# Copies between PSUM banks queued right behind their source product, and another order of the products in two blocks of a Strassen FFN

## The chip, the cores and the metric

The kernel runs on one core of one Trainium2 chip. Its five engines work side by side, each through its own queue in the order in which the program issued: TensorE (PE; its weight loads are shown as PEld), VectorE (DVE), ScalarE (ACT), GpSimd (POOL) and SyncE (SP), which issues most DMAs. They wait for each other by semaphores. Matmul results land in PSUM, in banks of 512 float32 columns; everything else that an engine touches lies in SBUF. The metric is the time of one execution on the device in microseconds, lower is better. A kernel's time is the median of its runs.

## The reference

One decoder block for 512 tokens of width 2048 in float32: RMSNorm, one input projection, 16 attention heads of two kinds, a group norm, an output projection, then the part that the change touches, a SwiGLU feed-forward of 5632 hidden units, and a final norm.

```python
hn2 = rmsnorm(h, norm2_g[l])
h = h + (jax.nn.silu(hn2 @ w_gate[l]) * (hn2 @ w_up[l])) @ w_down[l]
return rmsnorm(h, final_g)
```

## The kernel before

**Three matmuls for one.** Float32 accuracy is kept by splitting each operand into a high part and a low part and multiplying high by high, low by high and high by low. On the weight side a half of a unit (128 partitions by 512 columns) is one *job*. `first` (L133) is ScalarE's copy into `wh` (L139), `second` (L141) VectorE's subtract into `wl` (L142). `wh` and `wl` have five buffers each. Some jobs have a `prep`, an add of VectorE ahead of `first` (L786), or a `post` behind `second`: an add, or the issue of a load. `next_half` (L177) is called by every half just before its matmuls; it issues the split three halves ahead (`first` of job i+3, `second` of job i+2), then whatever `later(n, f)` (L188) has put off to this half. A piece of work that is put off is therefore queued behind the splits that were issued before it.

**The FFN.** The hidden units are worked in 44 blocks `f` of 128. For each block the gate and up projections of the 512 tokens are computed together by a Strassen scheme: instead of eight products there are seven, P1 to P7, each of 256 columns and two halves, 24 matmuls (`product`, L1037). A product's weights are sums of the quarters A11, A21, A22, A12 of the block's weights; the sums are made in place by VectorE, two 512-column adds each. P1 and P7 use PSUM tag "proj", P4 and P6 "sc", P5 "o". P2 adds into P1's bank and P3, from block 1 on, into P6's bank. Two banks are seeded, from block 1 on: before P6 runs, ScalarE copies P1 into P6's bank (L1084), and before P7 runs, it copies P6 into P7's bank (L1090). The seeded products then accumulate on top, so their first matmul waits for the copy.

**The order.** `ORDER` (L831) is P1, P4, P6, P5, P7, P2, P3 for blocks 1 to 43; block 0 has `ORDER0`. The list `sched` (L842 on) fixes the order of all products. In every fourth block, 4 to 40, sixteen units `d` of the down projection follow its third to sixth product, four after each (`down`, L1115, 24 matmuls each, banks `pd` or P3's). The last four blocks' down projection is done in `last` (L1176).

**What a product leaves behind.** `after` (L1067) issues what must be done with a finished product. For blocks from 1 on it is put off by one half (L1174), so it is queued in the second half of the product that follows. After P3 come two VectorE operations (L1109, L1112 with the add of L1073) and `finish`: Silu on ScalarE (L1057), a multiply by VectorE (L1060), a copy by ScalarE (L1061) and a subtract (L1065). After P2 comes a multiply out of P1's bank (L1104), after P7 a copy (L1100) and two VectorE operations (L1073, L1076).

**Around blocks 1 and 2.** After P5 in block 1 and in block 2, eight halves in a row each issue one `put_away` (L1134): VectorE multiplies a tile of the residual (L1135), and SP stores its 256 KB to DRAM (L1136). In blocks 41 and 42 the tiles are brought back (L1146). The raw weights have five buffers of a quarter each; the load of a quarter of the next block is issued by the post of P6, of P7 (two) or of P3 (L819 to L822) and starts when the buffer it gets is free.

**Two offsets.** `wh` and `wl` of a half start 16 columns into their buffers, or 32 for halves marked `even` (L122); in the FFN that is the first half of P1 in blocks 1, 2 and those with f % 8 = 5 (L827).

Of the kernel before, what the change touches and what calls it, by code (L numbers as in the profile page):

```python
# [13 lines left out]
AF = mybir.ActivationFunctionType  # L14
# [57 lines left out]
def block_kernel(ctx: ExitStack, tc: tile.TileContext, xt, wst, wdn, smalls, wg, w2c, bias, ident_in, out):  # L72
# [3 lines left out]
    pe, act, dve, pool_e, sp = nc.tensor, nc.scalar, nc.vector, nc.gpsimd, nc.sync  # L76
# [28 lines left out]
    def load_to(n):  # L105
        while state["dma"] < min(n, len(units)):
            u = state["dma"]
            t = wp.tile([128, 1024], F32, tag="raw", name="raw", bufs=RB)
            for k in range(2 if u < TWO else 1):
                c = slice(512 * k, 512 * k + 512) if u < TWO else slice(0, 1024)  # L110
                sp.dma_start(t[:, c], wst[u][:, c])
            raws[u] = t
            state["dma"] += 1
            if units[u] == ("quad", 0, 1):
                pool_e.dma_start(t, wst[u + 1], accum_op=OP.add)
# [72 lines left out]
    def later(n, f):  # L188
        i = len(lag)
        while i and lag[i - 1][0] > pos["half"] + n:  # L190
            i -= 1
        lag.insert(i, (pos["half"] + n, f))
# [65 lines left out]
    def tokens(*accs):  # L258
        return [[a[:, 128 * t:128 * t + 128] for a in accs] for t in range(accs[0].shape[-1] // 128)]
# [46 lines left out]
    for k in range(KB):  # L306
        x = xc.pop(k)
# [417 lines left out]
    for j in range(NH):  # L725
# [9 lines left out]
        o = {}  # L735
# [42 lines left out]
    def quad_jobs(f, order):  # L778

        u = base_u + 4 * f  # L780

        def q(i, k):
            return raws[u + i][:, 512 * k:512 * k + 512]

        def comb(o, x):
            return lambda: dve.tensor_tensor(o(), o(), x(), op=OP.add)  # L786

        def fetch(o, i, k):

            return lambda: pool_e.dma_start(o(), wst[u + i][:, 512 * k:512 * k + 512], accum_op=OP.add)  # L790

        def nxt(i):
            return lambda: load_to(u + 4 + i + 1)

        r = {}
        for k in range(2):
            A11, A21, A22, A12 = (lambda i=i, k=k: q(i, k) for i in range(4))

            if f == 0:
                r["P1", k] = Job(A11, load=None if k else nxt(-1), post=fetch(A11, 1, k))  # L800
                r["P5", k] = Job(A21, post=fetch(A21, 0, k))
                r["P7", k] = Job(A11)
                r["P2", k] = Job(A12)
                r["P4", k] = Job(A22, prep=comb(A12, A21))
                r["P6", k] = Job(A21)
                r["P3", k] = Job(A12)
            else:
                r["P1", k] = Job(A11, post=comb(A11, A21))
                r["P4", k] = Job(A22, post=comb(A21, A22))
                r["P6", k] = Job(A22, prep=comb(A22, A11))  # L810
                r["P5", k] = Job(A21)
                r["P7", k] = Job(A11)
                r["P2", k] = Job(A12)
                r["P3", k] = Job(A12, prep=comb(A12, A22))
        if f + 1 < FB:
            if f == 0:
                r["P6", 1].post = nxt(2)
                r["P3", 1].post = nxt(3)
            else:  # L819
                r["P6", 1].post = nxt(0)  # L820
                r["P7", 1].post = nxt(2)
                r["P3", 1].post = nxt(3)  # L822
        else:
            r["P6", 1].post = lambda: load_fin(1)
            r["P5", 1].post = lambda: load_fin(2)
            r["P3", 1].post = lambda: load_fin(LA)
        r["P1", 0].even = f in (1, 2) or f % 8 == 5  # L827
        return [r[p, k] for p in order for k in range(2)]

    ORDER0 = ("P1", "P5", "P2", "P7", "P4", "P6", "P3")  # L830
    ORDER = ("P1", "P4", "P6", "P5", "P7", "P2", "P3")  # L831

    def dn_job(p, nb):
        return Job(lambda: dn[p, nb], post=load_dn)

# [5 lines left out]

    sched = []  # L842
    for f in range(FB):
        qj = quad_jobs(f, ORDER if f else ORDER0)
        p = f // PH - 1
        nb = 0
        for i, name in enumerate(ORDER if f else ORDER0):
            sched.append(("q", f, name))
            jobs += qj[2 * i:2 * i + 2]
            if f and f % PH == 0 and i > 1:  # L850
                for _ in range(4):
                    if nb < KB:
                        sched.append(("d", p, nb))
                        jobs.append(dn_job(p, nb))
                        nb += 1
# [84 lines left out]
    def ft(name="ft"):  # L940
        return ffn.tile([128, S], F32, tag="ft", name=name, bufs=2)
# [82 lines left out]
    for n in range(8):  # L1024
# [4 lines left out]
    banks = {n: ps.tile([128, 512], F32, tag=t, name=n, bufs=2)  # L1029
             for n, t in (("P1", "proj"), ("P7", "proj"), ("P4", "sc"), ("P6", "sc"), ("P3", "t"))}  # L1030
# [4 lines left out]
    st = {}  # L1035
# [31 lines left out]
    def after(f, name):  # L1067

        def x(k):
            return st[k][:, :256]  # L1070

        def add(o, a, b):
            dve.tensor_tensor(o, a, b, op=OP.add)  # L1073

        def sub(o, a, b):
            dve.tensor_tensor(o, a, b, op=OP.subtract)  # L1076

        g, u = st.get("g"), st.get("u")
        if name == "P1":
            st["g"] = ft()  # L1080
            if f:
                st["u"] = ft()
                st["P6"] = banks["P6"]
                act.activation(x("P6"), x("P1"), AF.Copy)  # L1084
            else:
                act.activation(st["g"][:, LO], x("P1"), AF.Copy)
        elif name == "P6":
            if f:
                st["P7"] = banks["P7"]
                act.activation(x("P7"), x("P6"), AF.Copy)  # L1090
                act.activation(u[:, LO], x("P4"), AF.Copy)
                return
            add(g[:, HI], g[:, LO], x("P6"))
            dve.tensor_tensor(g[:, LO], x("P1"), st["r2"][:, LO], op=OP.mult)
            add(u[:, LO], g[:, HI], x("P7"))
            add(u[:, HI], u[:, LO], x("P5"))
            sub(u[:, LO], u[:, LO], x("P4"))
            add(g[:, HI], g[:, HI], x("P5"))
        elif name == "P7":
            act.activation(g[:, HI], x("P5"), AF.Copy)  # L1100
            sub(u[:, LO], x("P7"), u[:, LO])
            add(u[:, HI], x("P7"), g[:, HI])
        elif name == "P2":
            dve.tensor_tensor(g[:, LO], x("P1"), st["r2"][:, LO], op=OP.mult)  # L1104
            if f == FB - 1:
                finish(f, g, u, LO)
        elif name == "P3":
            if f:
                add(g[:, HI], x("P6"), g[:, HI])  # L1109
            else:  # L1110
                add(g[:, HI], g[:, HI], x("P3"))
            dve.tensor_tensor(g[:, HI], g[:, HI], st["r2"][:, HI], op=OP.mult)  # L1112
            finish(f, g, u, HI if f == FB - 1 else slice(0, 512))
# [28 lines left out]
    def bring_back(nb):  # L1142
        if nb == 0:
            st["dnp"].close()
            st["hs"] = ctx.enter_context(tc.tile_pool(name="fin", bufs=1)).tile([128, KB, S], F32, name="hs")
        sp.dma_start(st["hs"][:, nb, :], kept_sums[nb])  # L1146

    for kind, a, b in sched:
        if kind == "d":
            down(a, b)  # L1150
            continue
        f, name = a, b
        product(f, name)
        if name == "P5" and f in (1, 2):
            for n in range(8):
                later(n, lambda nb=8 * (f - 1) + n: put_away(nb))
        if name == "P5" and f in (FB - 3, FB - 2):
            for n in range(8):
                later(n, lambda nb=8 * (f - FB + 3) + n: bring_back(nb))
        if f == 0:  # L1160
            if name == "P7":
                r = st["rs2"] = Rsqrt(tokens(sacc), D, rab.v[:, :4])
                r.invert()
                dve.tensor_tensor(r.z, r.z, rab.y[:, :4], op=OP.mult)
                later(1, lambda r=r: st.update(inv=Spread(r.z, True), r2=Spread(r.y)))
            if name == "P6":
                st["inv"] = st["inv"](False)
                act.activation(st["rs2"].rs[:, 7, :1], ones[:, :1], AF.Silu)
                st["r2"] = st["r2"](tag="t", bufs=2)
                st["u"] = ft()  # L1170
            if name in ("P1", "P6", "P3"):
                later(0 if name == "P1" else 1, lambda name=name: after(0, name))
        elif name in ("P1", "P6", "P7", "P2", "P3"):
            later({(FB - 1, "P2"): 0, (FB - 1, "P3"): 3}.get((f, name), 1), lambda f=f, name=name: after(f, name))  # L1174
# [150 lines left out]
```

## Time and profile before

| | us |
|---|---|
| median of 3 runs | 2255.78 (2252.54 to 2259.78) |
| the profiled execution | 2250.55 |
| its span, first to last instruction | 2248.7 |
| from P1 of block 1 to P1 of block 4 | 71.38 |
| from P1 of block 4 to the last matmul of the blocks | 1258.16 |

How the lines are read: a group has its line, engine, operation, what it writes and reads, the count, then the engine's busy time and the mean duration, then the idle time of the engine before it and what ended most of that. In the waits a row says who waited for whom, for how long in total, how many times, and the longest. In the timeline a row is start, duration, engine, line, operation; square brackets give the idle time before it and what ended it. In a table by windows a row is the window, its length, then for each engine busy time and number of instructions, the granted TensorE clock, the share of the DMA engines and GB/s. Ends of matmuls are modelled; their starts are not.

### The profile page before, as it was taken

Reading aid. Unit: us, or ns where it says so; the run is one execution under the profiler, and the core shown is the slowest. Engines: PE = TensorE matmul, PEld = TensorE weight load, DVE = VectorE, ACT = ScalarE, POOL = GpSimd, SP = SyncE. Lnnn points to the kernel's source line nnn. Section 1 sums busy time; section 2 is a strip of 40 time slices with the busy share of each in tenths; the row PEclk is TensorE's granted clock in tenths of the full one; section 3 lists DMA queues with packets and bytes.
Section 4 is the critical chain, followed back from the end, with each engine's and each line's share of the span. In section 5 each row is a group of like instructions: output and inputs, shape, how many; then the busy total and the mean of one; then the engine's idle time right before and its main releaser. Section 6 shows DMA issues by size and latency. Waiting matters only on the chain.

```text
span 2248.7 us, 40167 instructions
## 1 busy us (share of the span) xinstructions
PE 2203.7 (98%) x15776; PEld 2058.1 (92%) x15776; DVE 1451.5 (65%) x2796; ACT 1080.5 (48%) x2155; POOL 181.4 (8%) x211
## 2 busy tenths in 40 slices
PE   9999999999999998999999999999999999999998
PEld 7888888888888888999999999999999999999997
DVE  6765555455667689758384856657484847667486
ACT  6544444344453455445454545445454545445456
POOL 0000000000000000010201011010202010010203
PEclk9999999999999999999999999999999999999999
DMA  6432222222224344572836465473737365463752
GB/s 226 161 119 82 87 78 75 97 78 87 78 94 154 100 104 140 137 166 94 176 111 148 120 151 131 124 160 98 172 107 177 104 146 137 124 140 100 158 194 94
DMA packets 109517, 282.64 MB, mean 126 GB/s; under 512 B 11920, under 2 KB 14608, under 8 KB 109328
## 3 DMA queue, kind: packets, MB, share of 16 engines
q1 hardware_dynamic: 85424, 236.49, 33.3%
q0 software_dynamic: 23760, 43.53, 12.7%
q8 instruction: 123, 2.02, 0.4%
q14 instruction: 66, 0.54, 0.1%
q10 hardware_dynamic: 144, 0.07, 0.0%
HBM read 229.70 MB, written 50.33 MB: 125 GB/s over the span
## 4 chain that ended last, share of the span: by engine, by line
PE 86%; DVE 7%; issue 4%; ACT 3%; ACTq 0%; DVEq 0%
PE P L1050 12%; PE P L1051 12%; PE P L1052 11%; PE pp L170 7%; PE pp L172 7%; PE pp L171 7%; PE pd L1050 4%; PE pd L1052 4%; PE pd L1051 4%; PE pab L170 3%; PE pab L171 3%; PE pab L172 3%; DVE wl L142 3%; DVE raw L786 1%; ACT wh L139 1%
## 5 line engine op out<-in xcount | busy, mean ns | idle before, releaser
L139 ACT ACTIVATE wh<-raw 128x512 fp32r<-128x512 f32 x888 | 545.5, 627 | 482.1 <-PE P L1051 185.0
L142 DVE TENSOR_TENSOR wl<-raw,wh 128x512 fp32r<-128x512 f32 x888 | 602.1, 687 | 176.8 <-ACT wh L139 170.5
L1050 PE MATMUL P<-ah,wh 128*128 128x256 f32 x1552 | 437.4, 282 | 31.2 <-ACT P L1084 30.9
L1052 PE MATMUL P<-ah,wl 128*128 128x256 f32 x1552 | 432.2, 279 | 0.0
L1051 PE MATMUL P<-al,wh 128*128 128x256 f32 x1552 | 432.0, 278 | 0.0
L1050 PEld LDWEIGHTS P<-ah,wh 128*128 128x128 f32 x1552 | 291.7, 188 | 39.3 <-ACT P L1084 39.2
L1052 PEld LDWEIGHTS P<-ah,wl 128*128 128x128 f32 x1552 | 292.2, 188 | 0.0
L1051 PEld LDWEIGHTS P<-al,wh 128*128 128x128 f32 x1552 | 291.8, 188 | 0.0
L142 DVE TENSOR_TENSOR wl<-rawd,wh 128x512 fp32r<-128x512 f32 x160 | 110.7, 692 | 265.9 <-ACT wh L139 259.5
L170 PE MATMUL pp<-ah,wh 128*128 128x512 f32 x640 | 260.5, 407 | 0.0
L172 PE MATMUL pp<-ah,wl 128*128 128x512 f32 x640 | 250.9, 392 | 0.0
L171 PE MATMUL pp<-al,wh 128*128 128x512 f32 x640 | 250.2, 391 | 0.0
L786 DVE TENSOR_TENSOR raw<-raw 128x512 f32<-128x512 f32 x346 | 238.2, 688 | 6.5
L1130 POOL DMA_DIRECT2D sums<-stg x160 | 138.6, 866 | 1150.3 <-ACT stg L1129 1042.7
L1050 PE MATMUL pd<-ah,wh 128*128 128x256 f32 x784 | 217.8, 278 | 0.0
L1052 PE MATMUL pd<-ah,wl 128*128 128x256 f32 x784 | 217.7, 278 | 0.0
L1051 PE MATMUL pd<-al,wh 128*128 128x256 f32 x784 | 217.5, 277 | 0.0
L139 ACT ACTIVATE wh<-rawd 128x512 fp32r<-128x512 f32 x160 | 100.8, 630 | 222.2 <-PE pd L1051 84.3
L1052 PEld LDWEIGHTS pd<-ah,wl 128*128 128x128 f32 x784 | 147.2, 188 | 0.0
L1051 PEld LDWEIGHTS pd<-al,wh 128*128 128x128 f32 x784 | 147.1, 188 | 0.0
L1050 PEld LDWEIGHTS pd<-ah,wh 128*128 128x128 f32 x784 | 147.1, 188 | 0.0
L172 PEld LDWEIGHTS pp<-ah,wl 128*128 128x128 f32 x640 | 120.2, 188 | 28.3 <-DVE wl L142 0.4
(284 smaller groups left out, 4631.2 us busy)
## 6 DMA issues: line engine op xcount, KB each, us to landing
raw<-in_wst_dram SPq DMA_DIRECT2D x310, 512.0 KB, 4.0
rawd<-in_wdn_dram SPq DMA_DIRECT2D x160, 256.0 KB, 3.1
sums<-stg POOLq DMA_DIRECT2D x160, 256.0 KB, 4.5
bias<-in_bias_dram SPq DMA_DIRECT2D x16, 320.0 KB, 3.0
xc<-in_xt_dram SPq DMA_DIRECT2D x16, 256.0 KB, 3.0
hs<-in_xt_dram SPq DMA_DIRECT2D x16, 256.0 KB, 5.2
sums<-hs SPq DMA_DIRECT2D x16, 256.0 KB, 2.1
hs<-sums SPq DMA_DIRECT2D x16, 256.0 KB, 5.4
```

The source lines that it names most:

```text
L139: act.activation(self.h, self.src(), AF.Copy)
L142: dve.tensor_tensor(self.l, self.src(), self.h.bitcast(F32), op=OP.subtract)
L170: pe.matmul(o, wh, mh, start=start, stop=False)
L171: pe.matmul(o, wh, ml, start=False, stop=False)
L172: pe.matmul(o, wl, mh, start=False, stop=stop)
L786: return lambda: dve.tensor_tensor(o(), o(), x(), op=OP.add)
L1050: pe.matmul(o, wh, mh, start=start, stop=False, skip_group_check=True)
L1051: pe.matmul(o, wh, ml, start=False, stop=False, skip_group_check=True)
L1052: pe.matmul(o, wl, mh, start=False, stop=stop, skip_group_check=True)
L1130: pool_e.dma_start(kept_sums[nb], t, accum_op=OP.add)
```

## The change

The two copies L1084 and L1090 leave `after`. They are issued in the loop over `sched` directly behind the matmuls of P1 and of P6, ahead of the next half's splits, instead of in the second half of the next product. `ft()` for `g` and `u` and the copy of P4 (L1091) stay where they were. Blocks 1 and 2 get an order of their own, in which P2 is third: P1, P4, P2, P6, P5, P7, P3. In it P6, P5 and P7 are two halves later than before, and with them what hangs on them: their posts, and the `put_away`s that start from P5.

```diff
     ORDER = ("P1", "P4", "P6", "P5", "P7", "P2", "P3")
+    ORDER1 = ("P1", "P4", "P2", "P6", "P5", "P7", "P3")
+
+    def order(f):
+        return ORDER0 if not f else ORDER1 if f < 3 else ORDER
...
-        qj = quad_jobs(f, ORDER if f else ORDER0)
+        qj = quad_jobs(f, order(f))
...
-        for i, name in enumerate(ORDER if f else ORDER0):
+        for i, name in enumerate(order(f)):
...
             if f:
                 st["u"] = ft()
-                st["P6"] = banks["P6"]
-                act.activation(x("P6"), x("P1"), AF.Copy)
...
         elif name == "P6":
             if f:
-                st["P7"] = banks["P7"]
-                act.activation(x("P7"), x("P6"), AF.Copy)
                 act.activation(u[:, LO], x("P4"), AF.Copy)
                 return
...
+        if f and name in ("P1", "P6"):
+            o = {"P1": "P6", "P6": "P7"}[name]
+            st[o] = banks[o]
+            act.activation(st[o][:, :256], st[name][:, :256], AF.Copy)
```

## The prediction

> **What bounds the kernel now.** I read the page first, then the waits of TensorE, then a window table by stage, then the timeline of one block.
>
> ```profile
> span 2248.7 us, 40167 instructions
> PE 2203.7 (98%) x15776; PEld 2058.1 (92%) x15776; DVE 1451.5 (65%) x2796; ACT 1080.5 (48%) x2155; POOL 181.4 (8%) x211
> PE 86%; DVE 7%; issue 4%; ACT 3%; ACTq 0%; DVEq 0%
> ```
>
> TensorE sets the end: 98% busy and 86% of the chain. So a gain can come only from TensorE idling less or from its matmuls following each other more closely. The waits of TensorE (whole span first, then blocks 1 to 3, then block 4 to the end of the FFN, the last row for the weight loads in that last stretch) name one thing:
>
> ```profile
> PE P L1050 <- ACT P L1084: 30.9, 35, 3.3
> ...
> PE P L1050 <- ACT P L1084: 8.7, 3, 3.3
> PE P L1050 <- DVE ft L1104: 0.8, 2, 0.4
> ...
> PE P L1050 <- ACT P L1084: 22.2, 32, 1.0
> PEld P L1050 <- ACT P L1084: 29.9, 37, 1.2
> ```
>
> L1084 is the copy of P1 into P6's bank. P6 waits for it in nearly every block. The ends of matmuls are modelled, so the truer loss from block 4 on is the 29.9 us of the weight loads. The other moved copy, L1090, is waited for by nobody. Why L1084 is late shows in the timeline of block 19 (ScalarE and TensorE rows; P4 follows P1 at 1415.48):
>
> ```profile
> 1415.48 0.28 PE L1050 MATMUL P<-T4h,wh 128*128 128x256 f32 x1
> 1415.77 0.63 ACT L1057 ACTIVATE ft<-ft 128x512 f32<-128x512 f32 x1 [1.29 <-DVE ft L1112]
> 1416.45 1.16 ACT L139 ACTIVATE wh<-raw 128x512 fp32r<-128x512 f32 x2
> 1418.44 0.63 ACT L1061 ACTIVATE ah<-ft 128x512 fp32r<-128x512 f32 x1 [0.84 <-DVE ft L1060]
> 1418.98 0.37 ACT L1084 ACTIVATE P<-P 128x256 f32<-128x256 f32 x1
> 1418.09 0.28 PE L1052 MATMUL P<-T4h,wl 128*128 128x256 f32 x1
> 1419.40 0.38 PE L1050 MATMUL P<-ah,wh 128*128 128x256 f32 x1 [1.04 <-ACT P L1084]
> ```
>
> P1 is complete at about 1415.65 (its last matmul's modelled end). The copy starts 3.3 us later, because it is queued behind the Silu of the block before, two weight splits and L1061, which itself waits for VectorE. P6 could have followed at 1418.20 and starts at 1419.40.
>
> The second thing is how closely matmuls follow each other. In this window table a row's x counts two matmuls that had begun before the window:
>
> ```profile
> 858.74:930.12 71.38, 61.83 (x504) 60.88 (x505) 63.34 (x109) 32.77 (x60) 0.00 (x0) 0.98 0.46 148
> 905.99:930.12 24.13, 21.51 (x168) 21.30 (x169) 19.63 (x33) 10.92 (x20) 0.00 (x0) 0.93 0.44 143
> 930.12:2188.28 1258.16, 1235.69 (x10562) 1228.16 (x10561) 806.09 (x1319) 613.74 (x1122) 138.62 (x160) 1.00 0.56 138
> 1442.57:1496.97 54.40, 54.40 (x482) 54.40 (x481) 21.71 (x34) 24.16 (x45) 13.87 (x16) 1.00 0.86 182
> 939.47:996.00 56.53, 56.53 (x482) 56.53 (x481) 22.10 (x35) 24.35 (x45) 13.87 (x16) 1.00 0.81 175
> 997.43:1001.51 4.08, 4.08 (x38) 4.05 (x36) 3.77 (x8) 2.60 (x5) 0.00 (x0) 1.00 0.20 36
> 1001.66:1015.90 14.24, 14.24 (x121) 14.24 (x121) 11.43 (x19) 7.56 (x14) 0.00 (x0) 1.00 0.49 148
> 2188.28:2216.50 28.22, 28.22 (x242) 28.22 (x241) 18.18 (x39) 23.10 (x50) 10.42 (x12) 1.00 0.18 56
> ```
>
> The same 480 matmuls (16 down units, P5, P7, P2, P3) take 54.40 us in block 20 and 56.53 us in block 4: 113.3 ns against 117.8 ns, at the full granted clock and without a wait in either. There are two spacings. In block 5 the first half of P1, the one that the kernel places at the other offset, ends the wide one: after it 36 matmuls take 4.08 us, 113.3 ns. P6 then waits, and the next 120 take 14.24 us, wide again. In the starts of all matmuls of the FFN I find no change of spacing except at a TensorE wait or at such a half; a start after a wait falls into the wide spacing about two times in three. So each P6 wait costs twice: the wait, and the chance of a wide stretch behind it.
>
> **The change part by part.** The sum is made against the profiled execution: 2250.55 us, that is the span of 2248.7 and 1.85 around it. The median of the runs shown is 2255.78, 5.2 above; I add nothing for that, since which spacing falls out after each wait may well be what differs from run to run.
>
> *P1's copy right behind P1 (43 blocks).* No instruction is added; one of 0.37 us moves forward on ScalarE past two splits and L1061. In block 19 ScalarE reaches it when Silu ends, 1416.40, P1 being complete; it is done at 1416.77. P6 can start at 1418.20, so 1.4 us are to spare. What now stands behind the copy (the two splits, 1416.45 to 1417.61, and through VectorE's subtract also L1060 and L1061) slides by 0.37; the half that needs the first of them is P6's second, due at 1418.20 + 1.36 = 1419.56. Both splits end at 1417.98, a subtract of 0.69 (the row of 1421.68 below) at 1418.7 at the latest. Covered by 0.9 us; without that cover it would cost its 0.37. VectorE's subtracts and L1065 behind it are as early or earlier than their users by as much. So from block 4 on P6 waits for nothing.
>
> The stretch from block 4 to the end of the FFN has 40 x 7 x 24 + 160 x 24 = 10,560 matmuls. At 113.3 ns they take 1196.8 us of the 1258.16: 61.4 us are waits (29.9 by the weight-load row) and wide spacing (the other 31.5; if all were wide it would be 10,560 x 4.44 ns = 46.9). With no wait left, the half in block 5 sets the close spacing and nothing in the trace ends it: close stretches run through whole down stretches in blocks 12, 16, 20, 24 and 28 while DMA share is 0.86. What remains: block 4, before that half, at two chances in three of 552 x 4.44 ns = 2.45, 1.6; some 1.8 for the offset halves and jitter. Gain 61.4 - 3.4 = **58.0**; bounds 30 (waits alone) and 61.4. The tail's first 240 matmuls inherit the spacing, now 28.22 / 240 = 117.6 ns: **1.0** more, between 0 and 1.0.
>
> *P6's copy right behind P6.* L1090 gains nothing, nobody waits for it. It costs ScalarE a wait at its place. Block 19, from the second half of P6 on (a window of VectorE work first, then rows):
>
> ```profile
> 1420.87:1427.67 6.80, 6.80 (x63) 6.80 (x61) 4.95 (x8) 3.74 (x7) 0.00 (x0) 1.00 0.64 173
> ...
> 1421.01 0.63 ACT L139 ACTIVATE wh<-raw 128x512 fp32r<-128x512 f32 x1 [0.60 <-PE P L1051]
> 1421.68 0.69 DVE L142 TENSOR_TENSOR wl<-raw,wh 128x512 fp32r<-128x512 f32 x1 [0.46 <-ACT wh L139]
> 1426.31 0.28 PE L1050 MATMUL P<-ah,wh 128*128 128x256 f32 x1
> ```
>
> The split at 1421.01 will stand behind a copy that starts when P6 ends, three halves of 1.36 before the last row, about 1422.3: it moves to 1422.7, 1.7 us, and its subtract ends at 1424.1. Its half, P7's second, starts at 1426.31: 2.2 us of cover. Queued behind it on VectorE are the subtracts and adds of P7 to P3; VectorE is idle 6.80 - 4.95 = 1.85 us up to 1427.67, which takes up the 1.7 before its full stretch begins. Cost 0; without that cover 1.7 a block.
>
> [...]
>
> *Blocks 1 and 2, P2 third.* Nothing is added; P6, P5 and P7 run two halves later, and with them the posts of P6 and P7, the put-aways (eight multiplies and eight 256 KB stores from P5 on) and the next block's loads. P2 accumulates in P1's bank and so needs the copy first. The loads by line (us to landing last), and SP's rows:
>
> ```profile
> raw<-in_wst_dram SPq DMA_DIRECT2D x310, 512.0 KB, 4.0
> ...
> 869.08 2.13 SPq L111 DMA_DIRECT2D raw<-in_wst_dram  x2
> 872.89 3.92 SPq L1136 DMA_DIRECT2D sums<-hs  x3
> 876.85 0.43 SPq L111 DMA_DIRECT2D raw<-in_wst_dram  x1
> ```
>
> The first load waits for A21's subtract in P5 as now, the second for A11's in P7, about 1 us later; the third now stands behind one store, not three. The second, issued near 872 (SP's two rows of 869.08 end at 871.2, and 1 us), lands 4.0 later near 876; it is A22 of block 2, whose half starts near 881: hidden. Blocks 1 and 2 now, Silu and P6's start:
>
> ```profile
> 864.21 0.63 ACT L1057 ACTIVATE ft<-ft 128x512 f32<-128x512 f32 x1 [1.28 <-DVE ft L1112]
> 867.84 0.39 PE L1050 MATMUL P<-ah,wh 128*128 128x256 f32 x1 [3.32 <-ACT P L1084]
> 887.54 0.63 ACT L1057 ACTIVATE ft<-ft 128x512 f32<-128x512 f32 x1 [1.88 <-DVE ft L1112]
> 888.12 0.28 PE L1052 MATMUL P<-T4h,wl 128*128 128x256 f32 x1
> 891.17 0.39 PE L1050 MATMUL P<-ah,wh 128*128 128x256 f32 x1 [2.77 <-ACT P L1084]
> ```
>
> In block 1 the split of P2 needs no add of VectorE ahead of it, as P6's did, so L1112 and Silu come one operation, 0.6 us, earlier: Silu ends at 864.84 - 0.6 = 864.2 and the copy at 864.6. P4's modelled end is 867.84 - 3.32 = 864.5, P2 could follow 0.17 before that, so 0.3 is left of the wait. In block 2 Silu stays ahead of the copy and VectorE far behind, and four put-aways now fall into P1 and P4 of blocks 2 and 3 where two did. Counting VectorE's queue at 0.6 us an operation, the copy ends about 1 us after P4 in block 2 and 1.7 after it in block 3, and a subtract behind the last put-aways costs 0.3 to 0.9 more in each: 2 us a block. So late next: VectorE. The sum over blocks 1 to 3: 71.38 us now, 504 x 113.3 ns = 57.1 at best, and not under VectorE's 63.34 busy us, which do not shrink. I take 64.4, near that floor because VectorE is what is full there: gain **7.0**, bounds 0 and 8.0. In it are L1104's 0.8 (P2's result is read early) and the half clock in block 3 (granted 0.93 in its row), which came behind a 2.62 us wait that becomes 1.7.
>
> Sum: 2250.55 - 58.0 - 1.0 - 7.0 = **2184.5 us**.
>
> **Rivals.** (1) The waits go but the spacing stays a lottery, or some small wait keeps resetting it: 2250.55 - 29.9 - 5.5 = 2215. For it: I know the spacing only by where it changes. Against it: close and wide stretches alike run on for 600 and more matmuls. [...] (2) The wide spacing holds throughout: 46.9 - 31.5 = 15.4 more, 2230; against it the offset half in block 5. (3) The change does not free P6, since the splits were as late as the copy: 2250. Against it: 35 waits in 43 blocks, so in eight of them P6 follows without one. (4) Slower: ScalarE held by P6's copy. It decides if the delayed subtract misses P7's second half (cover 2.2 us) or if VectorE's 1.85 us of idle time do not absorb it; then 43 x 1.7 = 73 come on top of (1): 2288. Against it: both covers exceed 1.7.
>
> **The numbers.** Forecast 0.64 (own range 2178 to 2193), (1) 0.17, (2) 0.08, (3) 0.04, (4) 0.03; 0.04 lie between forecast and (1). The range takes in the forecast, what lies between and (1): 2177 to 2222. A measurement of this kernel can tell 0.3% from no change; beyond that the forecast, (1), (2) and what lies between are faster, 0.93; (3) is 0.03 same after a part of it; slower 0.04.
>
> **What would show it.** Right: no TensorE wait on the copies from block 4 on; 480 matmuls in 54.4 us in every down stretch; Silu, then the copy, then two splits on ScalarE; about 2 us of waits in each of blocks 2 and 3, on VectorE's or ScalarE's account, and no half clock. Wrong: down stretches of 56.5 us (rivals 1, 2), P6 waiting for a subtract (3), P7 or P2 waiting for L139 or L142 (4).

## The result and the profile after

| | before | after |
|---|---|---|
| median, us (runs, range) | 2256.02 (4, 2252.54 to 2259.78) | 2191.44 (4, 2191.08 to 2192.62) |
| the profiled execution, us | 2250.55 | 2191.57 |
| from P1 of block 1 to P1 of block 4 | 71.38 | 62.58 |
| from P1 of block 4 to the last matmul of the blocks | 1258.16 | 1208.97 |
| the tail's first 240 matmuls | 28.22 | 27.29 |

The ratio is 0.9714, with an interval of 0.9698 to 0.9731. The three stretches differ by 8.80 + 49.19 + 0.93 = 58.92 us, and the spans by 58.9: there is no fourth place to look for.

The page of the changed kernel, its span, its engines and the head of its chain of waits:

```profile
span 2189.8 us, 40122 instructions
PE 2174.5 (99%) x15776; PEld 2036.3 (93%) x15776; DVE 1437.8 (66%) x2796; ACT 1066.6 (49%) x2155; POOL 181.3 (8%) x211
PE 97%; DVE 2%; issue 0%; ACT 0%; DVEq 0%; ACTq 0%
```

TensorE's share of the chain rose from 86 to 97%. But TensorE was *busy* for 29 us less, with the same 15,776 matmuls: matmuls that follow each other more closely are shorter in this column (480 of them 54.40 us in block 20 and 56.53 in block 4, in the table below), so part of the gain stands in the busy time, not in the idle time. The waits of TensorE from block 1 on, whole rows for the blocks:

```profile
PE P L1055 <- ACT P L1164: 1.6, 2, 1.0
PE P L1057 <- DVE wl L142: 0.7, 1, 0.7
```

L1164 is the new place of both copies. Of 30.9 us on L1084 remain 1.6, in two waits, and both are in blocks 2 and 3. Now the timeline of block 19 (the rows of ScalarE, then TensorE and VectorE):

```profile
1396.56 0.63 ACT L1062 ACTIVATE ft<-ft 128x512 f32<-128x512 f32 x1 [1.28 <-DVE ft L1113]
1397.10 0.37 ACT L1164 ACTIVATE P<-P 128x256 f32<-128x256 f32 x1
1397.40 1.13 ACT L139 ACTIVATE wh<-raw 128x512 fp32r<-128x512 f32 x2
...
1401.91 0.37 ACT L1164 ACTIVATE P<-P 128x256 f32<-128x256 f32 x1 [0.87 <-PE P L1057]
1402.20 1.14 ACT L139 ACTIVATE wh<-raw 128x512 fp32r<-128x512 f32 x2
...
1398.88 0.28 PE L1057 MATMUL P<-T4h,wl 128*128 128x256 f32 x1
1399.00 0.28 PE L1055 MATMUL P<-ah,wh 128*128 128x256 f32 x1
...
1402.85 1.29 DVE L142 TENSOR_TENSOR wl<-raw,wh 128x512 fp32r<-128x512 f32 x2 [0.92 <-ACT wh L139]
...
1405.80 0.28 PE L1055 MATMUL P<-ah,wh 128*128 128x256 f32 x1
```

Silu (L1062), then P1's copy, then two splits. The copy is done at 1397.47 and P6 follows P4 at 1399.00 without a gap: 1.5 us to spare. P6's copy at 1401.91 does make ScalarE wait (0.87 us, for P6), and the splits behind it and their subtracts are later. By the order of `next_half` the first split and the first of the two subtracts in the row of 1402.85 belong to P7's second half: that subtract ends at 1403.54 (1402.85 + 0.69), and the half begins at 1405.80, with 2.3 us to spare. The second subtract, done at 1404.14, is for P2's first half, one half later still.

The window table of the changed kernel: blocks 1 to 3; block 4 to the last matmul of the blocks; the down stretches of blocks 4 and 20; the 36 matmuls behind the offset half of blocks 5 and 13; the tail.

```profile
859.36:921.94 62.58, 60.30 (x504) 59.41 (x505) 61.64 (x109) 30.89 (x59) 0.00 (x0) 1.00 0.52 169
921.94:2130.91 1208.97, 1208.97 (x10562) 1208.97 (x10561) 794.10 (x1319) 600.67 (x1122) 138.63 (x160) 1.00 0.58 143
930.42:986.95 56.53, 56.53 (x482) 56.53 (x481) 21.90 (x35) 24.60 (x45) 13.86 (x16) 1.00 0.82 179
1420.76:1475.16 54.40, 54.40 (x483) 54.40 (x481) 21.73 (x34) 24.40 (x45) 13.88 (x16) 1.00 0.83 184
988.40:992.63 4.23, 4.23 (x38) 4.23 (x37) 3.40 (x7) 2.41 (x5) 0.00 (x0) 1.00 0.20 36
1237.16:1241.24 4.08, 4.08 (x39) 4.08 (x37) 3.31 (x7) 2.32 (x5) 0.00 (x0) 1.00 0.21 39
2130.91:2158.20 27.29, 27.29 (x244) 27.29 (x242) 18.00 (x39) 23.12 (x50) 10.43 (x12) 1.00 0.18 57
```

From block 4 on TensorE is busy for the whole 1208.97 us: no wait at all. Block 4 is wide (56.53), block 20 close (54.40); by the starts the down stretches of blocks 4, 8 and 12 take 56.5 us each and the seven from block 16 on 54.4. What was not forecast stands in the fifth row: behind the offset half of block 5, 36 matmuls take 4.23 us, 117.5 ns each, still wide. Behind block 13's they take 4.08, close, and from there to the end the starts are close, but for the offset halves. In blocks 1 to 3 the granted clock is 1.00.

Those blocks gained more than forecast. The rows that group VectorE's subtracts of the weights in them, before first:

```profile
L142 DVE TENSOR_TENSOR wl<-raw,wh 128x512 fp32r<-128x512 f32 x43 | 29.3, 686 | 6.7 <-ACT wh L139 6.3
```

```profile
L142 DVE TENSOR_TENSOR wl<-raw,wh 128x512 fp32r<-128x512 f32 x43 | 29.0, 688 | 0.4 <-ACT wh L139 0.4
```

Before, VectorE stood idle for 6.7 us ahead of these subtracts, while TensorE waited and ScalarE did its splits late; after it is 0.4. VectorE now fills 61.64 of the 62.58 us. Three of its rows in block 2, one operation right behind the other:

```profile
885.11 0.68 DVE L1136 TENSOR_TENSOR hs<-hs,prb 128x512 f32<-128x512 f32 x1
885.71 0.69 DVE L786 TENSOR_TENSOR raw<-raw 128x512 f32<-128x512 f32 x1
886.31 0.69 DVE L142 TENSOR_TENSOR wl<-raw,wh 128x512 fp32r<-128x512 f32 x1
```

In block 2 (ScalarE's and TensorE's rows) little is left:

```profile
884.62 0.63 ACT L1062 ACTIVATE ft<-ft 128x512 f32<-128x512 f32 x1 [3.72 <-DVE ft L1113]
885.16 0.37 ACT L1164 ACTIVATE P<-P 128x256 f32<-128x256 f32 x1
...
884.72 0.28 PE L1057 MATMUL P<-T4h,wl 128*128 128x256 f32 x1
885.58 0.38 PE L1055 MATMUL P<-B21h,wh 128*128 128x256 f32 x1 [0.58 <-ACT P L1164]
889.45 0.39 PE L1057 MATMUL P<-ah,wl 128*128 128x256 f32 x1 [0.65 <-DVE wl L142]
```

P2 waits 0.58 us for the copy, which stands behind Silu, which stood 3.72 us for VectorE; a subtract costs another 0.65.

### The profile page after: what moved, and what is told of

It reads as the page before. It is cut to its first block, busy times and chain, and to the rows that moved or that the text cites. A ratio compares the mean times of both kernels' runs of the same rounds, so it can differ in the third digit from the quotient of the medians.

```text
span 2189.8 us, 40122 instructions
## 1 busy us (share of the span) xinstructions
PE 2174.5 (99%) x15776; PEld 2036.3 (93%) x15776; DVE 1437.8 (66%) x2796; ACT 1066.6 (49%) x2155; POOL 181.3 (8%) x211
## 4 chain that ended last, share of the span: by engine, by line
PE 97%; DVE 2%; issue 0%; ACT 0%; DVEq 0%; ACTq 0%
PE P L1057 15%; PE P L1056 15%; PE P L1055 15%; PE pp L170 7%; PE pp L172 7%; PE pp L171 7%; PE pd L1056 4%; PE pd L1057 4%; PE pd L1055 4%; PE pab L170 3%; PE pab L172 3%; PE pab L171 3%; PE pt L541 1%; PE po L171 1%; PE psc L172 1%; PE po L170 1%
## 5 line engine op out<-in xcount | busy, mean ns | idle before, releaser
L1055 PE MATMUL P<-ah,wh 128*128 128x256 f32 x1552 | 430.0, 277 | 1.0 <-ACT P L1164 1.0
```

Source lines behind the costliest of these rows:

```text
L1055: pe.matmul(o, wh, mh, start=start, stop=False, skip_group_check=True)
```

## The experiments

Two theories stood against each other for what was missing from the forecast. A: moving P6's copy makes ScalarE wait, which costs time somewhere. B: the copies are free, and the missing time is the spacing from block 5 to block 12. The first four kernels take the change apart; the later ones go after the spacing.

**P1's copy alone.** P6's copy goes back to its old place; all else is as changed.

```diff
-        if f and name in ("P1", "P6"):
-            o = {"P1": "P6", "P6": "P7"}[name]
+        if f and name == "P1":
+            o = "P6"
...
         elif name == "P6":
             if f:
+                st["P7"] = banks["P7"]
+                act.activation(x("P7"), x("P6"), AF.Copy)
```

> The copy of P6 into P7's bank is put back to where it was before; the copy of P1 and the order of blocks 1 and 2 stay as changed. My theory: nobody waits for P6's copy in either place, so 2191 us as the changed kernel, within 3 us. Rival (ScalarE held by the copy that waits for P6's end costs TensorE time): faster than the changed kernel, by up to 1.7 us a block where it bites.

Measured: 2182.26 us (2181.67 to 2182.63), 0.9673 of before (0.9656 to 0.969): 9 us better than the change. Its windows, blocks 1 to 3 and block 4 to the end of the blocks:

```profile
858.37:920.86 62.49, 59.82 (x504) 58.89 (x505) 61.54 (x109) 30.70 (x59) 0.00 (x0) 1.00 0.53 169
920.86:2120.50 1199.64, 1199.64 (x10562) 1199.64 (x10561) 797.01 (x1319) 605.62 (x1122) 138.97 (x160) 1.00 0.59 144
```

Theory A seems to win, but the rows say otherwise. Neither kernel has a wait from block 4 on, and the 9.33 us (1208.97 - 1199.64) lie in blocks 5 to 12, where this kernel is close and the changed one wide. Blocks 1 to 3 are the same (62.49 and 62.58). What is left to explain is why block 5 ended the wide spacing here. The starts around the first half of P1 in block 5 (ns from one matmul to the next; the first three belong to block 4):

```
changed         119 117 118 120 120 125 117 118 120 120 125 117 118 120 122 118 118 117 118
P1's copy alone 117 119 115 116 119 119 121 116 118 120 120 120 120 120 121 113 113 114 113
```

In the changed kernel the offset matmuls fall into a beat of five (120 120 125 117 118) and the wide spacing goes on behind them. Here they settle at 120 and the close spacing follows.

**The copies without the new order** of blocks 1 and 2.

```diff
-        return ORDER0 if not f else ORDER1 if f < 3 else ORDER
+        return ORDER0 if not f else ORDER
```

> Both copies early, blocks 1 and 2 in their old order. Theory: from block 4 on as the changed kernel; in blocks 1 to 3 P6 has the third place again, its split needs VectorE's add, and P1 of blocks 2 and 3 waits for L1104 again: 1 to 4 us slower than the changed kernel, 2192 to 2196 us. If the wide spacing ends at another block, 10 us either way.

Measured: 2183.49 us (2183.26 to 2184.0), 0.9679 (0.9662 to 0.9696). Blocks 1 to 3 in its window table, then its waits of TensorE:

```profile
858.54:923.07 64.53, 60.50 (x505) 59.60 (x505) 62.48 (x109) 31.12 (x60) 0.00 (x0) 1.00 0.50 164
```

```profile
PE P L1055 <- DVE ft L1105: 3.3, 2, 1.6
...
PE P L1055 <- ACT P L1164: 0.7, 1, 0.7
```

The order is worth 1.95 us with the copies early (64.53 - 62.58): without it P1 of blocks 2 and 3 waits for L1105, the multiply that reads P2's result out of P1's bank, 1.6 us each. The copies do the rest of the 8.8. This kernel has P6's copy early and still ends the wide spacing in block 5, so that copy by itself does not keep block 5 wide, and no row from block 4 on shows a wait that it causes: theory A falls. Whether its place shifts the odds in block 5 is not shown.

**The new order without the copies.** Against the changed kernel: both copies back in `after`, with `ORDER1` kept.

```diff
+                st["P6"] = banks["P6"]
+                act.activation(x("P6"), x("P1"), AF.Copy)
...
+                st["P7"] = banks["P7"]
+                act.activation(x("P7"), x("P6"), AF.Copy)
...
-        if f and name in ("P1", "P6"):
-            o = {"P1": "P6", "P6": "P7"}[name]
-            st[o] = banks[o]
-            act.activation(st[o][:, :256], st[name][:, :256], AF.Copy)
```

> The order of blocks 1 and 2 alone, both copies as late as before. Theory: blocks 4 to 43 as before, blocks 1 to 3 a few us better: 2248 to 2256 us. Rival (the order carries the gain): near 2191.

Measured: 2256.62 us (2249.84 to 2259.0, 10 runs), 1.0001 (0.999 to 1.0012): no change. Its windows and the row of its waits:

```profile
858.87:931.77 72.90, 63.89 (x505) 63.30 (x505) 63.68 (x109) 32.13 (x59) 0.00 (x0) 0.93 0.46 145
931.77:2194.93 1263.16, 1242.47 (x10563) 1235.23 (x10561) 806.91 (x1319) 614.72 (x1122) 138.96 (x160) 1.00 0.56 137
```

```profile
PE P L1055 <- ACT P L1089: 29.4, 33, 3.5
```

Alone, the order helps nothing: blocks 1 to 3 take 72.90 against 71.38, and the granted clock is 0.93 over all three (0.98 before). The two parts of the change are not additive: the order is worth 1.95 with the copies and -1.5 without, by one execution of each. By the starts, 37 matmuls of blocks 1 to 3 ran at half the clock here, 213 ns apart, against 12 in the kernel before; those 25 more cost 2.5 us, more than the whole -1.5.

**The spacing mended, the wait left.** The kernel before, with P6's second half in every block at the other offset, so that an offset half stands right behind each wait.

```diff
         r["P1", 0].even = f in (1, 2) or f % 8 == 5
+        r["P6", 1].even = f > 0
```

> The kernel before, with the second half of P6 at the other offset in every block from 1 on. The waits for the copy stay. Theory: each wait costs twice, and the offset half takes the second cost away: wide spacing goes (31 us), less 0.08 us for each of 43 offset halves: 2225 to 2235 us. Rival (spacing has nothing to do with the offset half, or the wait alone matters): 2252 to 2260, unchanged.

Measured: 2236.29 us (2235.7 to 2240.12), 0.9917 (0.9894 to 0.994). Its windows and its wait row:

```profile
858.31:930.82 72.51, 62.13 (x505) 61.20 (x505) 63.06 (x109) 32.77 (x60) 0.00 (x0) 0.95 0.45 146
930.82:2176.06 1245.24, 1212.83 (x10562) 1204.97 (x10561) 804.65 (x1319) 613.06 (x1122) 138.97 (x160) 1.00 0.57 139
```

```profile
PE P L1051 <- ACT P L1085: 40.7, 38, 3.3
```

From the starts of all matmuls of the blocks (a spacing over 125 ns counted as a wait), the excess over 113.3 ns without a wait fell from 31.4 to 6.8 us, so an offset half does end the wide spacing most of the time. But the waits grew from 48.8 to 61.6 (40.7 us by this row's modelled ends, 30.9 before), 1.5 of it by more matmuls at half the clock in blocks 1 to 3. About half of the 24.6 us was given back. That fits a copy whose time is set by VectorE and ScalarE, so that a TensorE that comes sooner waits for longer; no run tested that by itself. By the starts from block 4 on, P6's first half was wide behind all 40 waits here, and behind 24 of 37 in the kernel before, so the chance of two in three is not a constant.

**Four waits put back.** The changed kernel, with P1's copy in its old place in blocks 14, 22, 30 and 38.

```diff
+    LATE = (14, 22, 30, 38)
...
             if f:
                 st["u"] = ft()
+                if f in LATE:
+                    st["P6"] = banks["P6"]
+                    act.activation(x("P6"), x("P1"), AF.Copy)
...
-        if f and name in ("P1", "P6"):
+        if f and name in ("P1", "P6") and not (name == "P1" and f in LATE):
```

> The changed kernel with the copy of P1 late again in blocks 14, 22, 30 and 38 alone. Theory: four waits of 1.2 us, and behind each, at two chances in three, a wide stretch that lasts until the offset half seven blocks later (1896 matmuls by 4.44 ns = 8.4 us): 2191 + 5 + 0 to 34, likeliest 2218 us. Rival (a wait costs only its own time): 2196.

Measured: median 2228.7 us (2211.64, 2228.51, 2228.88, 2229.06), 0.9869 (0.9824 to 0.9913). The profiled execution is the one of 2211.64, in which block 5 ended the wide spacing. Its windows and its wait row:

```profile
859.21:921.76 62.55, 60.38 (x504) 59.54 (x505) 61.60 (x109) 30.88 (x59) 0.00 (x0) 1.00 0.52 169
921.76:2149.43 1227.67, 1223.53 (x10562) 1222.75 (x10561) 793.95 (x1319) 601.10 (x1122) 138.61 (x160) 1.00 0.58 141
```

```profile
PE P L1056 <- ACT P L1091: 4.1, 4, 1.0
```

Four waits of about a microsecond cost 28 us in it (1227.67 - 1199.64 of the kernel with P1's copy alone). By the starts, 1.31 each is the wait, 5.2 together; the rest is wide spacing behind three of the four (14, 30 and 38, each up to the next offset half or to the end), while behind block 22 it stayed close. The two-in-three chance behind a wait, which the prediction read from before, is seen here in small (three of four). The other three runs are 17 us longer; block 5 left wide (9.3) and a fourth wide stretch, of 1,896 matmuls by 4.44 ns (8.4), would make 17.7, but no trace shows them.

**Longer offset stretches from block 4 on.** Both halves of P1 in blocks 4, 5 and 6 are offset, so that there are 24 matmuls to settle in and three tries.

```diff
-        r["P1", 0].even = f in (1, 2) or f % 8 == 5
+        r["P1", 0].even = f in (1, 2, 4, 6) or f % 8 == 5
+        r["P1", 1].even = f in (4, 5, 6)
```

> The changed kernel with both halves of P1 at the other offset in blocks 4, 5 and 6. Theory: the offset half in block 5 failed to end the wide spacing because its own spacing had not settled by its end; 24 matmuls are enough, so the close spacing starts at block 4: 9.5 us of blocks 5 to 12 and 2.2 of block 4 less, 2180 us. Rival (the spacing switches by chance or by something in block 13): 2191.

Measured: 2182.43 us (2181.91 to 2182.66), 0.9681 (0.9649 to 0.9713). Block 4 to the end of the blocks:

```profile
921.57:2121.51 1199.94, 1199.94 (x10563) 1199.94 (x10562) 793.23 (x1319) 600.40 (x1122) 138.63 (x160) 1.00 0.59 144
```

Block 4's 24 offset matmuls stayed in the beat of five throughout and left wide; block 5's settled and left close. So it worked through the second try, not the longer first one.

**No offset halves after block 2.**

```diff
-        r["P1", 0].even = f in (1, 2) or f % 8 == 5
+        r["P1", 0].even = f in (1, 2)
```

> The changed kernel without the offset halves from block 5 on. Theory: without waits nothing else ends a spacing, so the one that block 3 leaves holds to the end; if wide, 7896 matmuls from block 13 on and 240 of the tail by 4.44 ns, 36 us more: 2227 us (2182 if block 3 leaves the close one). Rival (the close spacing comes by itself once there are no waits): 2191.

Measured: 2227.36 us (2226.71 to 2228.12), 0.9881 (0.9854 to 0.9909). Its row:

```profile
921.21:2164.94 1243.73, 1243.73 (x10563) 1243.73 (x10561) 794.99 (x1319) 602.19 (x1122) 138.59 (x160) 1.00 0.58 139
```

No wait, the full clock, and 1243.73 / 10,560 = 117.8 ns to the end. This is rival (2) made real: without the later offset halves the change would have been worth 26 us (2253.47, the median of the kernel before beside it, less 2227.36), not 65.

**The changed kernel once more**, to see whether block 5 does the same every time.

> The changed kernel once more, beside the next two on the same chip. Theory: whether the offset half of block 5 ends the wide spacing is settled by how the starts stand when it begins, and that is nearly the same from run to run: 2191 us as before, with 117.8 ns up to block 13. Rival (chance in each run): some runs at 2182.

Measured: 2190.99, 2183.08, 2191.75 and 2182.79, median 2187.04, 0.9672 (0.9651 to 0.9694). The profiled execution is a long one (span 2189.2), with the same beat of five in block 5:

```profile
921.13:2130.11 1208.98, 1208.98 (x10563) 1208.98 (x10561) 793.78 (x1319) 600.50 (x1122) 138.62 (x160) 1.00 0.58 143
```

I had held that the outcome in block 5 belongs to the kernel. It doesn't: the same program gives two times, some 9 us apart, which is what blocks 5 to 12 are worth. So P1's copy alone is not shown to be a better kernel. It fell well in four runs of four and the changed kernel in two of eight; whether the place of P6's copy changes those odds, these runs are too few to tell.

**Two offset halves in a row**, in every block that has one.

```diff
+        r["P1", 1].even = f % 8 == 5
```

> The changed kernel with both halves of P1 at the other offset in blocks 5, 13, 21, 29 and 37, nothing else. Theory: in block 5 the spacing needs more than one half to settle; with two it settles and the close spacing starts at block 5: 9.5 us less, 2182 us. Rival (another half of block 4 or 6 did it in the run with more offset halves): 2191.

Measured: 2191.85, 2182.65, 2182.0, 2182.48 and 2183.05, median 2182.65, 0.9657 (0.9644 to 0.9671). The profiled execution is the long one; its stretch from block 4 on, and the 36 matmuls behind the two halves of block 5:

```profile
921.89:2131.21 1209.32, 1209.32 (x10563) 1209.32 (x10561) 794.02 (x1319) 601.14 (x1122) 138.64 (x160) 1.00 0.59 143
988.34:992.61 4.27, 4.27 (x38) 4.27 (x37) 3.41 (x7) 2.42 (x5) 0.00 (x0) 1.00 0.18 32
```

24 offset matmuls, and the wide spacing still goes on. The theory that one half is too short to settle in falls.

**The stores spread out.** P1's copy alone, with one put-away every second half from block 1 on (both blocks' worth of them), where the change has eight in a row twice; and a second offset half in block 5.

```diff
-        if name == "P5" and f in (1, 2):
-            for n in range(8):
-                later(n, lambda nb=8 * (f - 1) + n: put_away(nb))
+        if name == "P5" and f == 1:
+            for n in range(KB):
+                later(2 * n, lambda nb=n: put_away(nb))
...
+        r["P1", 1].even = f == 5
```

> Put together: P6's copy late, two offset halves in block 5, and the sixteen put-aways from P5 of block 1 on in every second half instead of two bursts of eight. Theory: the 3.8 us of waits left in blocks 2 and 3 come from VectorE's bursts; spread, most of them go: 2178 to 2181 us. Rival (VectorE's work in blocks 1 to 3 is the same in sum, so the waits only move): 2182.

Measured: 2181.13, 2179.94, 2190.16 and 2178.59, median 2180.54, 0.9657 (0.9636 to 0.9678). Blocks 1 to 3 and the waits:

```profile
859.13:920.54 61.41, 59.67 (x504) 59.04 (x505) 60.58 (x108) 30.61 (x59) 0.00 (x0) 1.00 0.49 164
```

```profile
PE P L1056 <- DVE ft L1108: 1.1, 1, 1.1
PE P L1056 <- ACT P L1094: 0.6, 1, 0.6
```

About a microsecond of blocks 1 to 3 is gained (61.41 against 62.49). The waits on P1's copy are gone, and others take their place: P7 of block 2 waits for its own copy of P6, which stands in its old place here (L1094), and P1 of block 4 for the multiply out of P2's result (L1108). One run of the four is long again.

**Spread stores and a try in every early block.** As the last, with one offset half in each of blocks 1 to 7 and none of two.

```diff
-        r["P1", 0].even = f in (1, 2) or f % 8 == 5
+        r["P1", 0].even = 0 < f < 8 or f % 8 == 5
```

> The kernel with spread put-aways and P6's copy late, with one offset half at the first half of P1 in each of blocks 1 to 7 in place of the two in block 5. Theory: an offset half that begins in the wide spacing ends it in part of the cases only, whatever its length, so separate tries in a row make it sure: all runs within 2 us of 2179, none at 2190. Rival (the same phase is met again in each block, so that where one fails all fail): a share of the runs at 2190 as before.

Measured: 2181.13 us (2178.47, 2180.64, 2181.13, 2181.17, 2181.74), 0.9671 (0.9657 to 0.9684). Its windows:

```profile
858.37:919.79 61.42, 59.66 (x504) 58.97 (x505) 60.65 (x108) 30.72 (x59) 0.00 (x0) 1.00 0.48 164
919.79:2119.97 1200.18, 1199.68 (x10560) 1199.49 (x10561) 798.55 (x1320) 606.14 (x1122) 138.96 (x160) 1.00 0.59 145
```

None of five runs is long. That is not proof that separate tries are surer: with two long runs in the nine of the last two kernels, five short ones in a row would still come more than once in four times by chance. The trace shows the tries at work once: block 4's half set the close spacing, a new wait in block 4 (0.5 us for ScalarE's L1132) ended it, and block 5's half set it again. The halves of blocks 6 and 7 began in the close spacing, so no failed try followed by a good one is seen here; the run with offset halves in blocks 4, 5 and 6 shows one. By its median it is 10 us under the first four runs of the change and 6 under the second four, and 74 under before.

## Why the prediction was right, and where it was not

The time is in the forecast's own range, 6.9 us above its middle. Two errors pull against each other in it, 8.8 us too much on the spacing and 1.8 too little on blocks 1 to 3. Which side of the middle the time fell on was chance: all first four runs were long, and the short outcome, near 2183, lies in the range as well. By its terms:

- **P1's copy and the waits.** Right, and shown by taking it away (four waits came back in just the four blocks, 14, 22, 30 and 38) and by doing it without P6's copy. The 29.9 us on the copies from block 4 on are gone. The slack of 1.4 us was 1.5. No split behind the copy came late.
- **The spacing from block 4 on.** The term of 58.0 measured 49.2. The term that was mis-sized rests on the step "the half in block 5 sets the close spacing and nothing ends it". Its second part held: with no wait, no close stretch ended in any trace here. Its first part is chance: block 5's offset half ended the wide spacing in some executions and not in others of the same program. It cost blocks 5 to 12, 9.3 us; of the sign "480 matmuls in 54.4 us in every down stretch" the stretches of blocks 4, 8 and 12 failed. Two small terms nearly cancel: block 4 was wide for 2.5 rather than the mean of 1.6, and the offset halves and jitter took 0.4, not 1.8 (1199.64 - 1196.8 - 2.45 in the kernel with P1's copy alone). 9.3 + 0.9 - 1.4 = 8.8.
- **The tail.** 1.0 forecast, 0.93 measured: it takes over the spacing that the blocks leave (27.29 / 240 = 113.7 ns).
- **P6's copy.** 0 forecast; blocks 1 to 3 are 0.1 us apart with and without it, and from block 4 on neither kernel waits; only with the stores spread out did a wait of 0.6 us on the copy in its old place appear. The cover of 2.2 us was 2.3.
- **Blocks 1 to 3.** 7.0 forecast, 8.8 measured, above the bound of 8.0. The bound was VectorE's 63.34 busy us, "which do not shrink". They did, to 61.64, with the same 109 operations. In block 2, VectorE's operations of 0.69 us started 0.60 apart when one stood right behind the other, so a full queue is shorter in busy time than the same work with gaps: the durations add up to 69.2 us before and 69.4 after, of which 6.1 and 7.6 overlap. That VectorE is the limit there was right (61.64 of 62.58), as was its consequence: less VectorE work in a row gained again (61.41). The waits left were forecast at 2 us each in blocks 2 and 3; by the starts, counted as above, they are 1.8 and 1.5. The 0.3 left in block 1 was 0.2. The half clock is gone, as forecast (granted 1.00); but before, it (12 matmuls, 213 ns apart) had followed the 2.62 us wait of block 3 and not the longer ones of blocks 1 and 2 (3.32 and 2.77), so that a shorter wait would avoid it was no safe inference.

The rivals. (1), a lottery of spacing at small waits, 2215: there was no small wait left from block 4 on, but a lottery at the offset halves there was, at a price of 9.3 us and not of 31.5. In the trace of before every offset half that began wide ended it, but only two of them, in blocks 5 and 37, had no wait at their start: few to take as sure, with close and wide stretches both running on for hundreds of matmuls. Without a wait, the stretches of blocks 4 to 43 are at 113.3, 117.8 or, in offset halves, about 120 ns. (2), wide throughout, 2230: not so, but the kernel without later offset halves shows that its price was right, 2227.36. (3), P6 not freed, fell: 35 waits went. (4), ScalarE held by P6's copy: held it was, by the row of 1401.91 (0.87 us for P6, with splits behind it), but that cost nothing, by the 2.3 us of slack ahead of P7's second half.

Left open: what decides at an offset half that begins in the wide spacing. The starts differ from its first matmuls on. Thirty halves or pairs of halves in P1 began wide and without a wait, over all traces but the one with P6's offset halves. The four that failed begin 118 120 120 125 or 117 121 120 124; of the 26 that ended it none has a spacing over 121 in its first twelve. That looks like a phase against something that runs beside it, which is a guess: no experiment changed such a phase alone. That the runs of before vary by 7 us fits the same cause, behind 35 waits; it is not shown.

## What to carry to other kernels

On an engine that works its queue in order, as ScalarE did here (0.87 us for P6, with splits behind it), put the operation that a later matmul waits for right behind its source, and put what has slack behind it: that was worth 30 us of waits here, though the operation takes 0.37 us. Then look at starts of matmuls from one to the next, not only at idle time: in the trace with four waits put back, each cost 1.3 us itself and 5.7 on average by the slower spacing that it left. Where two spacings exist, several separate chances for the stream to fall into the better one are worth trying (here they gave five short runs of five, too few to call them sure), and judge two versions by enough runs to see both outcomes of each.

## What was not expected of the hardware

- Matmuls of one shape, at the full granted clock, without a wait and with the same instructions, run at 113.3 or at 117.8 ns a start, and stay there: at 113.3 for 2,100 matmuls in a row between two offset halves of the changed kernel, at 117.8 for all 10,560 of blocks 4 to 43 without later offset halves. The difference over those 10,560 is 47 us.
- A run of matmuls whose weights stand at another offset goes at a mean of about 120 ns a start and can end the slower spacing. Begun in the close one, it left the close one in all 46 cases of the traces. Begun in the wide one, it either settled at an even 120 or fell into a beat of five of the same mean, and in that it stayed for as long as 24 matmuls. The same program did either from one run to the next.
- A TensorE with closer spacing gave about half its gain back in longer waits for a copy on ScalarE: 24.6 us of spacing gained, 12.8 us more waiting (1.5 of it half clock) in the kernel with the spacing mended and the wait left.
